# Branch b's projection as a seven-product Strassen multiplication

## The chip, the cores and the metric

The kernel runs on one core of one Trainium2 chip. The metric is the device time of one execution in microseconds (us), the median of several runs. The engines are named as in the profile: PE is the matrix engine (TensorE), PEld its weight load, DVE the vector engine, ACT the scalar engine, POOL the GpSimd engine, SP the engine whose queue issues most loads.

## The reference

One layer of a token mixer with a channel mixer, on 512 latent tokens of width 1024, with 256 context tokens that only feed the starting states of a gated linear attention. Cut to what matters here:

```python
u, vs, q, r, ga, gb, k, v, lr = _split(h @ w_in, IN_SPLITS)
a = _spatial_gating(gelu(u), gelu(vs), sgu_ln_g, sgu_ln_b, sgu_w, sgu_b)
o, s_f, s_b = _gla_bidir(...)                                   # 512 x 1024, 4 heads
o = o * rsqrt(mean(o * o) + EPS)                                # per head
o = o.reshape(...) * gla_norm_g                                 # one gain per column
ob = o * silu(r)
merged = sigmoid(ga) * (a @ w_br_a) + sigmoid(gb) * (ob @ w_br_b)
x = x + g1x * (merged @ w_o)
hx2 = _modulate(_rms_norm(x, norm2_g), sh2x, sc2x)              # h * (1 + scale) + shift
x = x + g2x * _conv_ffn(hx2, ...)
```

`sh2x`, `sc2x`, `g1x` and `g2x` are columns of `silu(c) @ w_ada + b_ada`, called modulations. Everything is in 32-bit floats.

## The kernel before, in words

**Precision.** Each operand of a large product is split into a high part (rounded by ACT, as `wh`, `ah`, `mh`) and a remainder (by DVE, as `wl`, `al`, `ml`), and each product is three matmuls: high by high, high by remainder, remainder by high. A weight tile is 128 x 1024: two row blocks of 512 columns, or eight row blocks of 128.

**Stages.** After the attention, the kernel runs one large product after another on PE: `u`, then `vs` (the shift branch of the spatial gating), gate a (`ga`), branch a's projection (`w_br_a`), gate b (`gb`), gate r (`r`), branch b's projection (`w_br_b`), the output product (`w_o`), then the channel mixer. Within each, tokens come in four tiles of 128 and columns in two halves `hf` of 512.

**Two ways to multiply 512 x 1024 by 1024 x 1024.** `wide_tm` is the plain way: for one column half, all four token tiles, then token tile by token tile for the other half (`wide_step`, L462). `strassen` (L517) splits tokens, inner dimension and columns in halves and makes seven products of quarters in the order a11, s3, s2, a12, s1, a22, s4, where s1 to s4 are sums of quarters of the left operand. Each of the seven takes two weight tiles, for two token tiles each; after each weight tile it calls `step()`, so steps 1 to 14 stand for the 14 weight tiles. `done(hf, t, source, sign)` is called for each finished output tile: (0, 0) and (0, 1) after a12, (1, 2) and (1, 3) after s1, (0, 2) and (0, 3) after a22, (1, 0) and (1, 1) after s4. With `low_first`, a12 comes after a22. In this kernel `vs`, `ga`, `gb`, `r` and `w_o` are Strassen products and `w_br_b` is a plain one.

**Weights.** `specs` is the list of weight tiles in the order of use, `loads` their DMAs; `weights(lead, ahead)` hands out the next tile, splits up to `lead` tiles further and issues loads up to `ahead` tiles further. `w_cols` is a plain tile; with `scaled` it is multiplied by the norm's gain `gng` while it is split (L201 on ACT, L202 on DVE). `w_strassen` makes the 14 tiles of a Strassen product, whose weight quarters also have to be added: `tt` holds b22 + b12, summed by an accumulating DMA from POOL (L230); t2 adds b11 to it (L274, L276 on DVE), and t4 adds b21 by a second accumulating DMA. There are five buffers each for raw weights, `wh` and `wl`.

**Around branch b.** `r_done` makes `ob` as `silu(r)` times the normalized attention output `os_` and puts a `turn` on a list `todo`: four transposes on PE (L1456), a copy on ACT and a remainder on DVE (L431, L432). `br_b_done` multiplies a finished tile by gate b, adds branch a (L1563, L1564) and puts an `mg_turn` on the list: four transposes (L1535), then the quarter sums s1 to s4 of the merged operand that `w_o`'s Strassen product needs, each split. `do()` takes turns from the list at chosen steps.

**Modulations.** `ada2` makes a modulation vector: 256 KB tiles of `w_ada` are multiplied by a column of `c` and added up on DVE (L1318), 16 such steps for each of scale, shift and the two gates; then PE sums over the partitions (L1337 for columns). It is a generator; `sc_tick` runs one piece of the second modulation's scale at a chosen step. Eight of its 16 sums run in `vs`, and the other eight and the column sums in branch b.

Pools: `heap` has 44 tiles of 128 x 512, `late` 27, PSUM two pools (`mm`, `gl`) of four banks. Instructions are put in order on each engine by a scheduler at compile time that follows the order of the program unless an operand isn't ready in its own plan of the times.

Of the kernel before, what the change touches and what calls it, by code (L numbers as in the profile page):

```python
# [8 lines left out]
F32 = mybir.dt.float32  # L9
# [7 lines left out]
P = 128  # L17
# [16 lines left out]
def backbone_kernel(  # L34
# [19 lines left out]
    def nm(s):  # L54
        cnt[0] += 1
        return f"{s}_{cnt[0]}"
# [10 lines left out]
    def mm():  # L67
        return pm.tile([P, 512], F32, tag="mm", name=nm("mm"))
# [110 lines left out]
            V.tensor_tensor(hl[1].tiles[i], part, hl[0].tiles[i].bitcast(F32), op=ALU.subtract)  # L179
        return hl  # L180

    def w_cols(w, c0, n=P, k0=0, kn=KT, scaled=False, ahead=False):
        ap = w[k0 * P:(k0 + kn) * P, c0:c0 + n].rearrange("(k p) c -> p k c", p=P)
        held = []

        def load():
            held.append(raw_tile(kn, n))
            dma(held[0], ap)
            last_load["cols"] = traced()[-1].name

        def split():
            if ahead:
                return split_heap(held.pop())
            if not scaled:
                return split_new(held.pop(), kn, n)
            raw = held.pop()
            wh = wp.tile([P, kn, n], F32R, tag="wh", name=nm("wh"))
            wl = wp.tile([P, kn, n], F32R, tag="wl", name=nm("wl"))
            for kk in range(kn):
                g_ = gng[:, k0 + kk:k0 + kk + 1]  # L200
                A.mul(wh[:, kk, :], raw[:, kk, :], g_)  # L201
                V.scalar_tensor_tensor(wl[:, kk, :], raw[:, kk, :], g_, wh[:, kk, :].bitcast(F32), op0=ALU.mult,  # L202
                                       op1=ALU.subtract)
            return wh, wl

        loads.append((len(specs), load))
        specs.append(split)

    def w_wide(w, scaled=False):
        for hf in range(2):  # L210
            for k in range(KT // 2):
                w_cols(w, hf * 512, 512, 2 * k, 2, scaled)

    def w_strassen(w, c0, add_b12=False, low_first=False, pool=heap):

# [23 lines left out]
        def load_t(j):  # L239
            def load():  # L240
                tt[j] = [pool([P, 512], s="tt") for _ in range(2)]
                start = len(traced())
                for kk in range(2):
                    dma(tt[j][kk], blk(1, 1, j)[kk * P:(kk + 1) * P, :])
                if low_first:
                    behind(start, last_load["cols"])
                add_rows(j, 0, 1)
            return load

# [75 lines left out]
            w_cols(w_br_a[0], hf * 512, 512, 2 * k, 2)  # L325
    w_strassen(wi, O_GB)
    w_strassen(wi, O_R)
    w_wide(w_br_b[0], scaled=True)
    w_strassen(w_o[0], 0, True, True, late)
    for f in range(FT):  # L330
        w_cols(ffn_w_up[0], f * P)
# [126 lines left out]
    def wide_step(ps, w, acts, t, k):  # L458
        wh, wl = w
        ah, al = acts(k, t)  # L460
        for i, (a, b) in enumerate(((ah, wh), (ah, wl), (al, wh))):
            T.matmul(ps, a, b[:, k % 2, :], start=(k == 0 and i == 0), stop=(k == KT - 1 and i == 2))  # L462

    def of_cols(acts):
        return lambda k, t: [z[:, t * P:(t + 1) * P] for z in acts[k]]

    def of_blocks(acts):
        return lambda k, t: [z[:, (k % 4) * P:(k % 4 + 1) * P] for z in acts[t, k // 4]]

    def wide_half(hf, pss, acts, done, step, lead=4, ahead=AHEAD):  # L470
        for k2 in range(KT // 2):
            w = weights(1, ahead)
            for kk in range(2):
                for t in range(4):
                    wide_step(pss[t], w, acts, t, 2 * k2 + kk)
                step()
            if k2:
                stream_split(pos[2] + min(k2 + 1, lead))
        for t in range(4):
            done(hf, t, pss[t])  # L480

    def wide_tm(acts, done, step, order=(0, 1, 2, 3)):

        wide_half(0, [mm() for _ in range(4)], acts, done, step)
        ws = [weights() for _ in range(KT // 2)]
        for t in order:
            ps = (mm if t != order[0] else gl)()
            for k in range(KT):
                wide_step(ps, ws[k // 2], acts, t, k)
            done(1, t, ps)  # L490
            step()
            step()

    def wide_all(acts, done, step):

# [804 lines left out]
    bc_g = {}  # L1300
    cols = {}

    ada_bank = [gl]

    def ada2(kinds):
        cs0 = {"g1": 2048, "sh": 3072, "sc": 4096, "g2": 5120}
# [108 lines left out]
    def ga_step():  # L1415
        slots[0] += 1
        n = slots[0] - 6
        if -3 <= n <= 0:
            vs_norm(n + 3)
        if 0 <= n < KT:  # L1420
            sgu_part(n)
        if n >= KT:
            a_split()
# [20 lines left out]
    wide_all(lambda k, t: [z[:, t * P:(t + 1) * P] for z in a_act[k]], br_a_done, br_a_step)  # L1444
    a_act.clear()
    ug.clear()
    ada_bank[0] = mm

    todo = []

    def turn(src, dst, key, bank, lo_pool=heap):

        def go():
            ps = bank()
            for kk in range(4):
                T.transpose(ps[:, kk * P:(kk + 1) * P], src[:, kk * P:(kk + 1) * P], ident)  # L1456
            dst[key] = split_act(ps, s="tr", eng=A.copy, lo_pool=lo_pool)
        return go

    def do(n=1):  # L1460
        for _ in range(n):
# [29 lines left out]
    for i in [i for i in traced()[start:] if i.engine == V.engine][:12]:  # L1491
        tc.add_manual_dep(i, low_banks[-1], mybir.DependencyInfo(
            mybir.DependencyClass.NoSync, mybir.DependencyReason.DATA), reason="low_banks")
    ada_bank[0] = gl

    ob = {}

    def r_done(hf, t, src, sign):
        sr = heap([P, 512], s="sr")
        A.activation(sr, src, AF.Silu, scale=sign)  # L1500
        V.tensor_tensor(sr, os_[t][hf], sr, op=ALU.mult)
        todo.append(turn(sr, ob, (t, hf), mm if hf == 0 and t < 2 or hf and t > 1 else gl))

    count = [0]

    def r_step():
        count[0] += 1
        if count[0] > 10:
            do()

    strassen(of_sums, r_done, r_step)
    hx.clear()
    sums.clear()
    do(len(todo) - 2)

    mg, mf = {}, {}

    def mg_turn(t, hf):

        s_, u, f_ = gb[t][hf], t % 2, lambda z: z.bitcast(F32)  # L1520

        def split(name, src, scale=1.0):
            hi, lo = heap([P, 512], F32R, s="mh"), heap([P, 512], F32R, s="ml")
            if scale == 1.0:
                A.copy(hi, src)
                V.tensor_tensor(lo, src, f_(hi), op=ALU.subtract)
            else:
                A.mul(hi, src, scale)
                V.scalar_tensor_tensor(lo, src, scale, f_(hi), op0=ALU.mult, op1=ALU.subtract)
            mg[name, u] = hi, lo  # L1530

        def go():
            ps = gl()
            for kk in range(4):
                T.matmul(ps[:, kk * P:(kk + 1) * P], s_[:, kk * P:(kk + 1) * P], ident, is_transpose=True,  # L1535
                         start=kk == 0, stop=kk == 3, skip_group_check=True)
            if t > 1 and hf == 0:
                mf["a21", u] = heap([P, 512], s="mf")
                A.copy(mf["a21", u], ps)
            elif hf == 0:  # L1540
                mf["a11", u] = heap([P, 512], s="mf")
                A.copy(mf["a11", u], ps)
                split("a11", ps)
                d = heap([P, 512], s="ms")
                V.tensor_tensor(d, ps, mf["a21", u], op=ALU.subtract)
                split("s3", d)
            elif t > 1:
                split("a22", ps)
                d, q = mf.pop(("a21", u)), mf["a11", u]
                V.tensor_tensor(d, ps, d, op=ALU.subtract)  # L1550
                V.tensor_tensor(q, q, d, op=ALU.add)
                split("s2", q, -1.0)
                split("s1", d)
            else:
                split("a12", ps)
                q = mf.pop(("a11", u))
                V.tensor_tensor(q, q, ps, op=ALU.subtract)
                split("s4", q)
        return go

    def br_b_done(hf, t, ps):
        s_ = gb[t][hf]
        V.tensor_tensor(s_, ps, s_, op=ALU.mult)  # L1563
        V.tensor_tensor(s_, s_, br[t][hf], op=ALU.add)  # L1564
        if hf:
            todo.append(mg_turn(t, hf))
        elif t > 1:
            todo.extend([mg_turn(t, 0), mg_turn(t - 2, 0)])

    count[0] = 0  # L1570

    def br_b_step():
        count[0] += 1
        if count[0] > 1:
            do()
        if 8 < count[0] < 12:
            stream_split(pos[2] + count[0] - 7)
        if count[0] < 5:
            for _ in range(2):
                sc_tick()  # L1580
        if count[0] == 7:
            for _ in range(3):
                sc_tick()

    wide_tm(of_blocks(ob), br_b_done, br_b_step, (2, 0, 3, 1))
    drain()
    am2 = const([P, 8], "am2")
    V.tensor_scalar(am2, cols["sc"], 1.0, None, op0=ALU.add)
    V.tensor_tensor(am2, am2, n2g, op=ALU.mult)
# [104 lines left out]
    def wo_step():  # L1694
        count[0] += 1
        if count[0] == 1:
            x1_load()
            table_for(AF.Sqrt)
        if count[0] == 14:
            low_later.append(later)  # L1700
            stream_split(pos[2] + 4)
            low_later.clear()
        do()

    strassen(lambda name, k, t: [z[:, k * P:(k + 1) * P] for z in mg[name, t]], wo_done, wo_step, True)


    gact, s12, s4 = [], [], []
# [373 lines left out]
```

## Time and profile before

| | |
|---|---|
| median of 3 runs | 908.41 us (907.97 to 908.92) |
| profiled execution, its own time | 908.53 us |
| its span, first to last instruction | 906.8 us |
| mean granted clock | 0.997 |
| PE busy | 892.1 us, 98% |
| DVE busy | 755.7 us, 83% |
| ACT busy | 477.4 us, 53% |
| POOL busy | 80.9 us, 9% |
| HBM read | 135.52 MB |

The span is the profiled execution from its first instruction to its last; the execution's own time is some 1.7 us longer. Stages by the start of their PE work: `vs` 249.6, gate a 290.0, branch a 335.3, gate b 378.8, gate r 419.8, branch b 460.6, `w_o` 510.5. In the rows of the profile, `out<-in` names the tile written and those read, `x12` is a count, and a bracket after a row is the idle time ahead of it and what ended it.

### The profile page before, as it was taken

The numbers are of one execution on the slowest core, as the hardware profiler recorded it, in microseconds if no ns is written. First come the engines' busy times: TensorE is split into PE (matmuls) and PEld (weight loads), VectorE is DVE, ScalarE is ACT, GpSimd is POOL, SyncE is SP. The second block draws the span as 40 slices with busy tenths as digits, with TensorE's granted clock in tenths as the row PEclk, the third lists the DMA queues.
The fourth block names the chain that finished last, engine by engine and source line by source line (L and its number), as shares of the span: only waits on it lengthen the run. The fifth ranks groups of instructions, "written<-read, shape, count | busy, mean of one in ns | idle before, by whom it ended". The sixth has DMA issues, their size and how long they took to land.

```text
span 906.8 us, 12638 instructions
## 1 busy us (share of the span) xinstructions
PE 892.1 (98%) x4527; PEld 745.7 (82%) x4527; DVE 755.7 (83%) x1312; ACT 477.4 (53%) x846; POOL 80.9 (9%) x114
## 2 busy tenths in 40 slices
PE   6999999999999999999999999999999999999996
PEld 5778888888888888888888889888888888888885
DVE  5668777899999778796686986899999888999796
ACT  5146454767465742475652568533333343466574
POOL 3000000001121010021020100000000000123003
PEclk9999999999999999999999999999999999999998
DMA  9961401026875668699576633263444333399522
GB/s 270 330 177 30 118 22 48 25 70 191 198 202 159 162 190 295 200 263 254 167 210 186 148 90 112 71 198 116 136 132 128 105 93 116 96 236 252 141 76 93
DMA packets 127068, 138.44 MB, mean 153 GB/s; under 512 B 7402, under 2 KB 82486, under 8 KB 127006
## 3 DMA queue, kind: packets, MB, share of 16 engines
q1 hardware_dynamic: 115197, 118.38, 41.3%
q0 software_dynamic: 10368, 18.57, 12.3%
q8 instruction: 35, 0.57, 0.3%
q10 hardware_dynamic: 1440, 0.69, 0.3%
q14 instruction: 28, 0.22, 0.1%
HBM read 135.52 MB, written 2.10 MB: 152 GB/s over the span
## 4 chain that ended last, share of the span: by engine, by line
PE 96%; DVE 2%; ACT 1%; DMA 0%; issue 0%; ACTq 0%; DVEq 0%
PE mm L439 29%; PE gl L517 12%; PE mm L462 9%; PE mm L517 9%; PE gl L1857 7%; PE mm L1857 5%; PE gl L439 4%; PE gl L462 3%; PE mm L454 3%; PE mm L762 3%; PE gl L982 2%; PE gl L762 1%; PE mm L1152 1%; PE mm L1091 1%; PE gl L685 1%; PE gl L1018 1%
## 5 line engine op out<-in xcount | busy, mean ns | idle before, releaser
L164 ACT CAST wh<-raw 128x1024 fp32r<-128x1024 f32 x107 | 111.8, 1051 | 105.2 <-PE mm L439 65.9
L165 DVE TENSOR_TENSOR wl<-raw,wh 128x1024 fp32r<-128x1024 f32 x107 | 130.0, 1219 | 21.1 <-ACT wh L164 19.3
L1740 DVE SCALAR_TENSOR_TENSOR cacc<-ca,ccol,cacc 128x441 f32<-128x441 f32 (+2 forms) x176 | 120.9, 693 | 6.1 <-ACT cacc L1728 2.8
L439 PE MATMUL mm<-h2h,wh 128*128 128x512 f32 x320 | 124.6, 389 | 0.0
L439 PE MATMUL mm<-h2h,wl 128*128 128x512 f32 x320 | 124.6, 389 | 0.0
L439 PE MATMUL mm<-h2l,wh 128*128 128x512 f32 x320 | 124.6, 389 | 0.0
L439 PEld LDWEIGHTS mm<-h2l,wh 128*128 128x128 f32 x320 | 60.1, 188 | 12.5
L439 PEld LDWEIGHTS mm<-h2h,wh 128*128 128x128 f32 x320 | 60.1, 188 | 12.4
L439 PEld LDWEIGHTS mm<-h2h,wl 128*128 128x128 f32 x320 | 60.1, 188 | 12.4
L1318 DVE SCALAR_TENSOR_TENSOR acc<-wa,c_col,acc 128x512 f32<-128x512 f32 x64 | 46.0, 747 | 4.6 <-DMA wa<-in_w_ada_dram 4.0
L1743 ACT ACTIVATE cacc<-cacc 128x512 f32<-128x512 f32 x22 | 13.9, 633 | 58.7 <-DVE cacc L1740 58.6
L230 POOL DMA_DIRECT2D tt<-in_w_in_dram x32 | 27.9, 998 | 174.5 <-DMA tt<-in_w_in_dram 57.5
L264 DVE TENSOR_TENSOR wl<-tt,wh 128x512 fp32r<-128x512 f32 x56 | 36.4, 683 | 7.6 <-ACT wh L263 7.6
L263 ACT CAST wh<-tt 128x512 fp32r<-128x512 f32 x56 | 32.6, 620 | 18.2 <-DVE tt L276 3.9
L517 PE MATMUL mm<-wh,hxh 128*128 128x512 f32 x96 | 38.0, 395 | 0.0
L517 PE MATMUL mm<-wh,hxl 128*128 128x512 f32 x96 | 37.4, 390 | 0.0
L517 PE MATMUL mm<-wl,hxh 128*128 128x512 f32 x96 | 37.4, 389 | 0.0
L1779 POOL DMA_DIRECT2D b<-in_ffn_w_down_dram x11 | 9.5, 888 | 283.4 <-DMA b<-in_ffn_w_down_dram 256.8
L1799 ACT CAST wh<-raw 128x1024 fp32r<-128x1024 f32 x22 | 23.1, 1053 | 15.9 <-PE mm L1857 4.7
L1800 DVE TENSOR_TENSOR wl<-raw,wh 128x1024 fp32r<-128x1024 f32 x22 | 26.8, 1218 | 4.5 <-ACT wh L1799 4.4
L517 PE MATMUL gl<-wh,xh 128*128 128x512 f32 x64 | 25.5, 399 | 0.0
L517 PE MATMUL gl<-wh,xl 128*128 128x512 f32 x64 | 24.9, 390 | 0.0
(552 smaller groups left out, 2398.0 us busy)
## 6 DMA issues: line engine op xcount, KB each, us to landing
raw<-in_w_in_dram SPq DMA_DIRECT2D x54, 512.0 KB
wa<-in_w_ada_dram SPq DMA_DIRECT2D x96, 256.0 KB
raw<-in_ffn_w_up_dram SPq DMA_DIRECT2D x44, 512.0 KB
raw<-in_ffn_w_down_dram SPq DMA_DIRECT2D x22, 512.0 KB
tt<-in_w_in_dram POOLq DMA_DIRECT2D x32, 256.0 KB, 6.8
tt<-in_w_in_dram SPq DMA_DIRECT2D x16, 256.0 KB
raw<-in_w_br_a_dram SPq DMA_DIRECT2D x8, 512.0 KB
raw<-in_w_br_b_dram SPq DMA_DIRECT2D x8, 512.0 KB
```

The lines of the kernel that those rows point to most:

```text
L164: A.copy(wh, raw)
L165: low = lambda: V.tensor_tensor(wl, raw, wh.bitcast(F32), op=ALU.subtract)
L230: G.dma_start(tt[j][kk], blk(kh, nh, j)[kk * P:(kk + 1) * P, :], accum_op=ALU.add)
L263: A.copy(wh[:, kk, :], tt[j][kk])
L264: V.tensor_tensor(wl[:, kk, :], tt[j][kk], wh[:, kk, :].bitcast(F32), op=ALU.subtract)
L439: T.matmul(ps, a[:, k, :], b[:, c0:c0 + n], start=(k == 0 and i == 0), stop=(k == KT - 1 and i == 2))
L462: T.matmul(ps, a, b[:, k % 2, :], start=(k == 0 and i == 0), stop=(k == KT - 1 and i == 2))
L517: T.matmul(ps[t], a, b[:, kk, :], start=(first and i == 0), stop=(j == 1 and kk == 1 and i == 2), skip_group_check=again)
L762: T.matmul(fps[i], a, b, start=(k == 0 and z == 0), stop=(k == KT - 1 and z == 2))
L1318: V.scalar_tensor_tensor(a_, w_, c_col[:, k:k + 1], a_, op0=ALU.mult, op1=ALU.add)
L1740: V.scalar_tensor_tensor(o, a_[:, r0 + dy:r1 + dy, c0 + dx:c1 + dx], wcol(tap), o, op0=ALU.mult, op1=ALU.add)
L1857: T.matmul(ps, a[:, t * P:(t + 1) * P], w[b][:, j, c0:c0 + n], start=(first and i == 0), stop=(last and i == 2), skip_group_check=again)
```

## The change

`w_br_b` becomes a Strassen product. Its weights are no longer scaled by the norm's gain: the gain is put on the turned operand, where its columns lie on the partitions. One new function, `sums_turn`, takes the place of `turn` and `mg_turn`: it transposes one quarter (a11, a22, a21 or a12, for token tile u), with the gain if one is given, and makes the splits of the quarters and sums s1 to s4 as soon as their parts are there. Both branch b and `w_o` take their operands from it. Turns run at steps 10 to 14 (a11, a11, a22, a22, both a21) of gate r and of branch b, and at step 5 (both a12) of the product that follows. The scale's remaining eight sums and its column sums move to steps 1, 2, 4, 5 and 6 of gate a. The later loads of `w_o`'s `tt` are put behind the last quarter of `w_br_b`.

```diff
-    w_wide(w_br_b[0], scaled=True)
+    w_strassen(w_br_b[0], 0)
...
     def ga_step():
         slots[0] += 1
         n = slots[0] - 6
+        for _ in range({1: 3, 2: 3, 4: 2, 5: 1, 6: 1}.get(slots[0], 0)):
+            sc_tick()
...
+    def sums_turn(dst, name, u, src, scale=None):
...
+        def split(n_, raw, c=1.0):
+            hi, lo = heap([P, 512], F32R, s="mh"), heap([P, 512], F32R, s="ml")
+            if c == 1.0:
+                A.copy(hi, raw)
+                V.tensor_tensor(lo, raw, f_(hi), op=ALU.subtract)
+            else:
+                A.mul(hi, raw, c)
+                V.scalar_tensor_tensor(lo, raw, c, f_(hi), op0=ALU.mult, op1=ALU.subtract)
+            dst[n_, u] = hi, lo
 
         def go():
-            ps = bank()
+            ps = mm()
             for kk in range(4):
                 T.transpose(ps[:, kk * P:(kk + 1) * P], src[:, kk * P:(kk + 1) * P], ident)
-            dst[key] = split_act(ps, s="tr", eng=A.copy, lo_pool=lo_pool)
+            raw = ps
+            if scale is not None or name in ("a11", "a22"):
+                raw = heap([P, 512], s="mf")
+                if scale is None:
+                    A.copy(raw, ps)
+                else:
+                    for kk in range(4):
+                        A.mul(raw[:, kk * P:(kk + 1) * P], ps[:, kk * P:(kk + 1) * P], scale[:, kk:kk + 1])
+            if name in ("a11", "a22"):
+                dst["raw", name, u] = raw
+                split(name, raw)
+            elif name == "a21":
+                q, d = kept("a11"), kept("a22")
+                s3 = heap([P, 512], s="ms")
+                V.tensor_tensor(s3, q, raw, op=ALU.subtract)
+                split("s3", s3)
+                V.tensor_tensor(d, d, raw, op=ALU.subtract)
+                V.tensor_tensor(q, q, d, op=ALU.add)
+                split("s2", q, -1.0)
+                split("s1", d)
+                dst["raw", "q", u] = q
+            else:
+                split("a12", raw)
+                q = kept("q")
+                V.tensor_tensor(q, q, raw, op=ALU.subtract)
+                split("s4", q)
         return go
...
-        V.tensor_tensor(sr, os_[t][hf], sr, op=ALU.mult)
-        todo.append(turn(sr, ob, (t, hf), mm if hf == 0 and t < 2 or hf and t > 1 else gl))
+        V.tensor_tensor(os_[t][hf], os_[t][hf], sr, op=ALU.mult)
+        todo.append(sums_turn(ob, *turn_names(hf, t), os_[t][hf], gng[:, 4 * hf:4 * hf + 4]))
...
+    turns = {10: 1, 11: 1, 12: 1, 13: 1, 14: 2}
...
-    def br_b_done(hf, t, ps):
+    def br_b_done(hf, t, src, sign):
         s_ = gb[t][hf]
-        V.tensor_tensor(s_, ps, s_, op=ALU.mult)
-        V.tensor_tensor(s_, s_, br[t][hf], op=ALU.add)
...
+        V.tensor_tensor(s_, src, s_, op=ALU.mult)
+        if sign > 0:
+            V.tensor_tensor(s_, br[t][hf], s_, op=ALU.add)
+        else:
+            V.tensor_tensor(s_, br[t][hf], s_, op=ALU.subtract)
+        todo.append(sums_turn(mg, *turn_names(hf, t), s_))
...
+    late_turns = {5: 2}
...
-        if count[0] < 5:
-            for _ in range(2):
-                sc_tick()
-        if count[0] == 7:
-            for _ in range(3):
-                sc_tick()
...
-    wide_tm(of_blocks(ob), br_b_done, br_b_step, (2, 0, 3, 1))
+    strassen(of_turned(ob), br_b_done, br_b_step)
```

More of the change, by code (lines that the diff above doesn't have):

```diff
@@ L180, in split_heap, with w_cols @@
         return hl
-    def w_cols(w, c0, n=P, k0=0, kn=KT, scaled=False, ahead=False):
+    def w_cols(w, c0, n=P, k0=0, kn=KT, ahead=False):
         ap = w[k0 * P:(k0 + kn) * P, c0:c0 + n].rearrange("(k p) c -> p k c", p=P)
@@ L193, in split @@
                 return split_heap(held.pop())
[L194 to L204, printed above, removed]
+            return split_new(held.pop(), kn, n)
         loads.append((len(specs), load))
         specs.append(split)
[L209 to L212, printed above, removed]
     def w_strassen(w, c0, add_b12=False, low_first=False, pool=heap):
@@ L245, in load @@
                 if low_first:
-                    behind(start, last_load["cols"])
+                    behind(start, last_load["b22"])
                 add_rows(j, 0, 1)
@@ L462, in wide_step @@
             T.matmul(ps, a, b[:, k % 2, :], start=(k == 0 and i == 0), stop=(k == KT - 1 and i == 2))
[L464 to L492, printed above, removed]
     def wide_all(acts, done, step):
@@ L1301, in backbone_kernel @@
     cols = {}
-    ada_bank = [gl]
+    ada_bank = [mm]
     def ada2(kinds):
@@ L1446, in backbone_kernel, with turn_names @@
     ug.clear()
-    ada_bank[0] = mm
     todo = []
-    def turn(src, dst, key, bank, lo_pool=heap):
+    ob, mg = {}, {}
+    def sums_turn(dst, name, u, src, scale=None):
+        f_ = lambda z: z.bitcast(F32)
+        kept = lambda n_: dst.pop(("raw", n_, u))
+        def split(n_, raw, c=1.0):
[7 more added lines that the diff above has]
+            dst[n_, u] = hi, lo
         def go():
-            ps = bank()
+            ps = mm()
             for kk in range(4):
                 T.transpose(ps[:, kk * P:(kk + 1) * P], src[:, kk * P:(kk + 1) * P], ident)
-            dst[key] = split_act(ps, s="tr", eng=A.copy, lo_pool=lo_pool)
-        return go
+            raw = ps
[24 more added lines that the diff above has]
+                split("s4", q)
+        return go
+    def turn_names(hf, t):
+        return (("a11", "a21"), ("a12", "a22"))[hf][t // 2], t % 2
     def do(n=1):
@@ L1493, in backbone_kernel @@
             mybir.DependencyClass.NoSync, mybir.DependencyReason.DATA), reason="low_banks")
-    ada_bank[0] = gl
-    ob = {}
     def r_done(hf, t, src, sign):
@@ L1500, in r_done @@
         A.activation(sr, src, AF.Silu, scale=sign)
-        V.tensor_tensor(sr, os_[t][hf], sr, op=ALU.mult)
-        todo.append(turn(sr, ob, (t, hf), mm if hf == 0 and t < 2 or hf and t > 1 else gl))
+        V.tensor_tensor(os_[t][hf], os_[t][hf], sr, op=ALU.mult)
+        todo.append(sums_turn(ob, *turn_names(hf, t), os_[t][hf], gng[:, 4 * hf:4 * hf + 4]))
     count = [0]
+    turns = {10: 1, 11: 1, 12: 1, 13: 1, 14: 2}
     def r_step():
         count[0] += 1
-        if count[0] > 10:
-            do()
+        do(turns.get(count[0], 0))
     strassen(of_sums, r_done, r_step)
@@ L1513, in backbone_kernel @@
     sums.clear()
[L1514 to L1559, printed above, removed]
@@ L1561, in br_b_done @@
-    def br_b_done(hf, t, ps):
-        s_ = gb[t][hf]
-        V.tensor_tensor(s_, ps, s_, op=ALU.mult)
-        V.tensor_tensor(s_, s_, br[t][hf], op=ALU.add)
[L1565 to L1568, printed above, removed]
+    def br_b_done(hf, t, src, sign):
+        s_ = gb[t][hf]
+        V.tensor_tensor(s_, src, s_, op=ALU.mult)
[4 more added lines that the diff above has]
+        todo.append(sums_turn(mg, *turn_names(hf, t), s_))
@@ L1570, in backbone_kernel @@
     count[0] = 0
+    late_turns = {5: 2}
     def br_b_step():
         count[0] += 1
[L1574 to L1577, printed above, removed]
-        if count[0] < 5:
-            for _ in range(2):
-                sc_tick()
-        if count[0] == 7:
-            for _ in range(3):
-                sc_tick()
-    wide_tm(of_blocks(ob), br_b_done, br_b_step, (2, 0, 3, 1))
-    drain()
+        do((turns if count[0] > 9 else late_turns).get(count[0], 0))
@@ L1587, in backbone_kernel @@
+    of_turned = lambda dst: lambda name, k, t: [z[:, k * P:(k + 1) * P] for z in dst[name, t]]
+    strassen(of_turned(ob), br_b_done, br_b_step)
+    ob.clear()
+    ada_bank[0] = gl
     am2 = const([P, 8], "am2")
@@ L1702, in wo_step @@
             low_later.clear()
-        do()
-    strassen(lambda name, k, t: [z[:, k * P:(k + 1) * P] for z in mg[name, t]], wo_done, wo_step, True)
+        do(late_turns.get(count[0], 0))
+    strassen(of_turned(mg), wo_done, wo_step, True)
     gact, s12, s4 = [], [], []
```

## The prediction

> **What bounds the kernel now.** I read the page's busy shares and its chain first, then the chain of branch b's stretch in order of time, then that stretch by windows.
>
> ```profile
> span 906.8 us, 12638 instructions
> PE 892.1 (98%) x4527; PEld 745.7 (82%) x4527; DVE 755.7 (83%) x1312; ACT 477.4 (53%) x846; POOL 80.9 (9%) x114
> PE 96%; DVE 2%; ACT 1%; DMA 0%; issue 0%; ACTq 0%; DVEq 0%
> ```
>
> PE is the bound: 98% busy, 96% of the chain. Only fewer PE instructions, or PE waits, can move the end. The chain from gate r to the output product w_o (start, length, what):
>
> ```profile
> 419.78 10.88 PE mm L517 x48
> 459.75 0.87 PE gl L1456 x8
> 460.62 2.06 PE mm L462 x9
> 462.68 0.04 issue
> 470.12 10.93 PE mm L462 x48
> 481.05 1.68 PE gl L1337 x16
> 491.07 0.87 PE gl L1535 x8
> 510.10 0.44 PE gl L1535 x4
> 510.54 3.68 PE mm L517 x16
> 528.09 10.90 PE gl L517 x48
> ```
>
> L517 is a Strassen product, L462 branch b's plain one, L1456 and L1535 the two kinds of turn, L1337 the scale's column sums. All of it is PE; the one wait is 0.04 us. 48 products last 10.88 us in Strassen form and 10.93 in plain form: 0.2267 us each. By windows (the stages shift norm vs, gate a, r, branch b, w_o; columns: length, PE, weight loads, DVE, ACT, POOL, granted clock, DMA share, GB/s), and last the densest DVE stretch of b and w_o:
>
> ```profile
> 249.62:289.98 40.36, 40.36 (x176) 32.60 (x175) 39.43 (x66) 23.59 (x37) 6.93 (x8) 1.00 0.69 189
> 289.98:335.32 45.34, 45.34 (x234) 38.71 (x233) 38.97 (x59) 31.15 (x45) 5.61 (x9) 1.00 0.57 164
> 419.78:460.62 40.84, 40.84 (x194) 33.99 (x193) 27.01 (x37) 26.83 (x42) 3.49 (x4) 1.00 0.67 189
> 460.62:510.54 49.92, 49.88 (x246) 41.42 (x245) 39.86 (x66) 20.65 (x37) 8.34 (x9) 1.00 0.66 168
> 510.54:549.20 38.66, 38.66 (x174) 31.89 (x174) 32.66 (x50) 25.48 (x42) 2.04 (x4) 1.00 0.47 132
> 491.83:524.49 32.66, 32.66 (x158) 27.18 (x157) 29.95 (x46) 19.59 (x34) 4.49 (x6) 1.00 0.47 114
> ```
>
> See two things: the clock is 1.00 throughout, and DVE is second everywhere. In vs it is 97.7% busy (39.43 of 40.36) and PE still waits for nothing; in b and w_o its densest stretch reaches 29.95/32.66 = 92%.
>
> **The change part by part.** Prices of single instructions (mean ns after the comma):
>
> ```profile
> L165 DVE TENSOR_TENSOR wl<-raw,wh 128x1024 fp32r<-128x1024 f32 x107 | 130.0, 1219 | 21.1 <-ACT wh L164 19.3 <-PE gl L1007 1.4
> L264 DVE TENSOR_TENSOR wl<-tt,wh 128x512 fp32r<-128x512 f32 x56 | 36.4, 683 | 7.6 <-ACT wh L263 7.6
> L202 DVE SCALAR_TENSOR_TENSOR wl<-raw,vec_b,wh 128x512 fp32r<-128x512 f32 x16 | 11.8, 747 | 6.4 <-ACT wh L201 6.4
> L1318 DVE SCALAR_TENSOR_TENSOR acc<-wa,c_col,acc 128x512 f32<-128x512 f32 x64 | 46.0, 747 | 4.6 <-DMA wa<-in_w_ada_dram 4.0 <-DVE acc L1318 0.2
> L201 ACT ACTIVATE wh<-raw,vec_b 128x512 fp32r<-128x512 f32 x16 | 11.4, 722 | 13.9 <-PE mm L462 8.6 <-issue 2.8 <-PE gl L517 1.7
> L1481 ACT ACTIVATE os<-o,var 128x256 f32<-128x256 f32 x16 | 7.3, 502 | 9.6 <-DVE acc L1318 9.6
> L431 ACT CAST trh<-mm 128x512 fp32r<-128x512 f32 x4 | 2.3, 567 | 0.0
> ```
>
> *1. The product.* Plain: 8 row blocks x 4 token tiles x 2 halves x 3 = 192 matmuls. Strassen: 7 products x 4 row blocks x 2 token tiles x 3 = 168. So 24 x 0.2267 = **-5.44 us**. In sentences the sum does not use: the Trainium skill (TensorE: Matmul & The Clock Gate, "Back-to-back issue gap") gives about 131 ns for a sustained 512-column matmul behind its weight load; by that the saving would be only about 3.1 us, an estimate from that page. The trace disagrees (48 in 10.88 us), so I keep 227 ns.
>
> *2. Turns and column sums.* Eight turns of branch b's operand and eight of the merged one stand before and after, four transposes each: 0.44 us for x4, 0.87 for x8, in either form. The column sums (1.68 us) move from b to gate a, where PE is as full. Both 0.
>
> *3. Scale sums in gate a.* Eight multiply-adds (L1318), two column copies, 16 column matmuls and eight 256 KB loads move there, on SP's queue ahead of later weights. Back to back a multiply-add takes about 0.67 us, 5.4 in all: DVE goes from 38.97 of 45.34 to 44.7 of 47.0, 95%, under the 97.7% that vs bears without a PE wait. The loads add 2 MB to a stage at 164 GB/s; vs took the same eight at 189. What waits anew is PE: the column matmuls stand at steps 5 and 6 right behind the last sums, with the gate's products queued behind them. Bounds 0 (the lead of the weights covers it) to 1 us; I take 0, being nearest to vs.
>
> *4. Weights of b.* Out: 16 scaled casts on ACT (L201) and 16 scaled remainders on DVE (L202). In: 14 weight tiles, four row sums on POOL's accumulating queue and four more later, 7 MB instead of 4. A direct precedent is the passage from gate b to r, the same weight scheme:
>
> ```profile
> 409.34 1.23 DVE L274 TENSOR_TENSOR raw<-raw,raw 128x1024 f32<-128x1024 f32 x1 [0.92 <-DMA raw<-in_w_in_dram]
> 417.80 1.29 DVE L264 TENSOR_TENSOR wl<-tt,wh 128x512 fp32r<-128x512 f32 x2 [0.74 <-ACT wh L263]
> 419.01 1.29 DVE L276 TENSOR_TENSOR tt<-tt,raw 128x512 f32<-128x512 f32 x2
> 423.24 1.29 DVE L264 TENSOR_TENSOR wl<-tt,wh 128x512 fp32r<-128x512 f32 x2 [0.98 <-ACT wh L263]
> tt<-in_w_in_dram POOLq DMA_DIRECT2D x32, 256.0 KB, 6.8
> SPq L224 <- DVE tt L276: 29.8, 4, 17.7
> ```
>
> r begins at 419.78, and by then the weight sums of its third product are made (409, 419) and their last remainder is done at 424.5; it is needed at 433. An accumulating load lands 6.8 us after issue and is asked for six weights (16 us) ahead. So DMA and POOL: 0, bounded above by one late load, 4.5 us.
>
> *5. The turn of the third quarter (a21), r's end.* PE makes two turns (0.87), then the first product (24 x 0.2267 = 5.44), then needs s3 of token tile 0 at +6.3 and of tile 1 at +7.7. The norm's scale costs four 128x128 multiplies on ACT: 256 columns cost 502, 512 cost 722, so 128 about 390, some 0.30 back to back, 1.3 us a turn. ACT: silu 0.5, four multiplies to 1.8, four to 3.1, casts of 0.57; DVE 0.6 apiece: both s3 are whole at about +5.4. If instead the queues run tile 0's three splits before tile 1's multiplies, tile 1 comes at +9.4 (remainder due +8.1): 1.3 us. I take 0, the merged operand's turns having left no wait at 510-528.
>
> *6. The last quarter (a12), step 5 of branch b.* Between its transposes and its use lie one step (2.72) plus the second turn (0.44): 3.16 us for tile 0, 4.5 for tile 1. ACT needs 0.5 + 1.3 + 0.57 = 2.4, then again 1.9: 4.3, plus up to 1.05 if a weight cast stands between. Bounds 0 to 1.0: I take **+0.5**.
>
> *7. DVE from r's last product to w_o's step 5.* PE: 0.87 + 38.1 + six turns at 0.44 = 41.6, then five steps and the turns before: 14.5; 56.1 us. DVE in that time, operations of 512 columns: gate r's last 2, a21 12, a12 6, t4 4, t2's remainders 4, Strassen adds 4, merge 16, the merged operand's a11, a22 4 and a21 12, w_o's first weights 8 and t2 8: 80. At 0.605 (two take 1.29) 48.4, and six of 1024 at 1.14, 6.8: 55.2. Four remainders (s1, a22) are due later: 52.8, or 94%. At vs's 97.7% that fits; at 92% it ends at 57.4, 1.3 late. I take **+0.8**. If t2's sums were not made early in r: 55.2 + 4 x 0.605 + 2 x 1.14 = 59.9, at 92% 65.1: 9.0 late. So 0 to 9.0. w_o's tail has 6 us of DVE to spare (32.66 of 38.66) for the seven operations that arrive later.
>
> **Sum:** -5.44 + 0.5 + 0.8 = -4.1. The profiled execution took 908.53 (906.8 and 1.7 outside the span), 0.12 over the median of 908.41: the forecast is **904.3**.
>
> **The rivals.** *A, everything is covered:* 908.41 - 5.44 = 903.0. For it: no PE wait anywhere from gate b to w_o now, and vs at 97.7%. Against: steps 6 and 7 each lack about 1 us at their upper ends.
>
> *B, the turns run in tile order:* 1.3 at r's end, the same at w_o's start, 1.0 at step 6: -5.44 + 3.6, 906.6. For it: ACT has eight multiplies more at r's end than today. Against: early work fills gaps, as at 419.01.
>
> *C, slower: DVE falls behind in branch b.* One mechanism: t2's sums are not made in r but inside b, so the s2 and a12 operands of w_o come late at step 5. Full price -5.44 + 9.0: 912.0. It decides when DVE is more than 7.2 us late there; from 3.6 it eats the gain. For it: the ledger's 94 to 107%. Against: r leaves DVE 27.01 of 40.84, and the precedent made the sums early. A PE gap would also cost clock by the Trainium skill (same page, "The HAM clock gate"): about 3.4 us of idling halves it, by estimate up to 1.7 us more; no run here shows such a gap, and the rows read 1.00.
>
> *D, branch b's weights come late:* raw buffers are freed by DVE, and SP's queue stands behind them (29.8 us in four waits). One late load: 904.3 + 4.5 = 908.8, same or just slower. Against: those waits cost PE nothing today.
>
> **How the numbers follow.** Forecast 0.40, A 0.23, B 0.13, C 0.14, D 0.10. 0.2% (1.8 us, 906.6 and 910.2) is about what a measurement of this kernel tells from no change. Faster: 0.40 + 0.23 + most of B, 0.11 = 0.74. Same: 0.02 of B, 0.06 of C where it stops short, 0.05 of D: 0.13. Slower: 0.08 + 0.05 = 0.13. The range goes from A less 0.2 to just short of D, 902.8 to 908.4, leaving out C and most of D; the likeliest case alone is 903.6 to 905.4.
>
> **What would show it.** L462 in branch b gone, 168 matmuls of L517 in its place in about 41 us with turns. The chain between r and w_o all PE but for under 2 us, lying at the seventh weight of branch b (ACT, a12) and in w_o's second or third product (DVE). Gate a longer by 1.7 us of column sums with no PE wait; DVE near 95% in gate a, branch b and w_o's first half. Wrong if PE waits over 3.6 us for DVE in w_o (C), if a wait on a weight tile whose releaser is a DMA shows (D), or if w_o's tail ends late because DVE is.

## The result and the profile after

The changed kernel takes 914.43 us (median), the kernel before 908.66 us on the same chip: 1.0064 of it, 95% interval 1.0052 to 1.0076, so 5.8 us slower (4.7 to 6.9 by that interval). The PE work shrank as forecast, and PE stood still for longer than it saved. The page of the changed kernel, its first lines and its chain:

```profile
span 912.1 us, 12690 instructions
PE 890.6 (98%) x4503; PEld 740.1 (81%) x4503; DVE 775.4 (85%) x1340; ACT 496.7 (54%) x894; POOL 88.1 (10%) x122
PE 43%; DVE 3%; ACT 2%; DMA 1%; issue 0%; DVEq 0%; ACTq 0%
```

4527 PE instructions became 4503: the 24 matmuls are gone. But the chain, 96% PE before, now leaves PE. Followed back from the end, it stays with PE as far as w_o; from there back it alternates between PE and long DVE stretches, and it begins at a load issued at 459 us. Two pieces of it in order of time (start, length, what), branch b's start and w_o's. Line numbers are those of each kernel's own file. In this one L472 is a matmul of a Strassen product and L1425 a turn's transposes; L1415, L1416, L1418 and L1419 split a quarter or a sum of the operand; L1440, L1442 and L1443 make s3, s1 and s2; L248, L249 and L261 are the cast, the remainder and t2's sum of a weight tile `tt`; L490 is the copy of a PSUM bank behind the product s2.

```profile
459.19 7.47 DMA tt<-in_w_br_b_dram
466.65 0.02 issue
466.68 1.14 ACT wh L248 x2
467.82 0.53 ACT mh L1415
468.35 0.02 issue
468.37 0.69 DVE ml L1416
...
512.28 0.60 DVE ms L1440
512.87 0.60 DVE mf L1442
513.47 0.60 DVE tt L261
514.08 0.60 DVE ml L1416
...
518.29 0.61 DVE ms L1440
518.90 0.02 issue
518.92 0.63 ACT mh L1415
```

Branch b starts at 464.4, and a row sum of its weights (`tt`) lands only at 466.7. In w_o, s3 of token tile 0 (`ms` L1440) is made at 512.3 and that of tile 1 at 518.3, with the rest of tile 0's turn and four operations on weights (`tt`, `wl`) in between. The stages by windows (vs, gate a with its sums, r, branch b, w_o; columns as in the prediction):

```profile
250.31:290.51 40.20, 40.20 (x176) 32.42 (x174) 39.18 (x65) 23.51 (x37) 6.93 (x8) 1.00 0.76 209
290.51:339.11 48.60, 47.38 (x250) 40.39 (x248) 44.44 (x71) 31.15 (x45) 5.27 (x8) 1.00 0.62 179
423.57:464.41 40.84, 40.84 (x194) 33.76 (x192) 27.25 (x35) 28.39 (x52) 7.01 (x8) 1.00 0.67 167
464.41:509.34 44.93, 42.98 (x204) 34.51 (x202) 43.45 (x67) 33.34 (x65) 9.33 (x10) 1.00 0.85 222
509.34:553.40 44.06, 41.38 (x180) 31.85 (x177) 41.88 (x66) 30.72 (x51) 4.46 (x6) 1.00 0.60 149
```

The stages meet at the first instruction of the next stage's product here; w_o ends at the first transposes of the second norm (553.40; 549.04 before). Against the kernel before:

| stage | before | after | difference | what it is |
|---|---|---|---|---|
| gate a | 45.33 | 48.60 | +3.3 | 1.7 column sums moved in, 1.4 a wait, the rest gaps beside them |
| gate b, gate r | 81.7 | 81.8 | 0 | |
| branch b | 49.91 | 44.93 | -5.0 | 5.4 fewer matmuls, 1.7 column sums out, 0.4 a turn out; 2.6 lost in waits |
| w_o | 38.75 | 44.06 | +5.3 | 0.4 a turn in; 4.9 in waits and in products out of order |
| norm and first channel-mixer products | 26.69 | 27.83 | +1.1 | a wait of 0.8 for DVE, with its gap 1.0 |

The differences add up to 4.8 us. The profiled executions differ by 5.3 (913.82 against 908.53); `vs` begins 0.7 us later in the changed one (250.31 against 249.62), behind work that the change does not touch.

What PE waited for between 285 and 560 us, the four largest of seven rows (in total, times, longest), and the largest of the waits for the copy L490:

```profile
PE mm L472 <- ACT mh L1415: 2.1, 2, 1.2
PE gl L472 <- ACT gl L490: 1.4, 2, 1.0
PE mm L1292 <- ACT vr L1344: 1.2, 1, 1.2
PE gl L1571 <- DVE yt L1587: 0.8, 1, 0.8
531.71 0.50 PE L472 MATMUL gl<-wh,mh 128*128 128x512 f32 x1 [1.03 <-ACT gl L490]
```

ACT is named in three, but read the rows of ACT and DVE too. At the longer of the two waits for `mh` (1.2 us, w_o) ACT had itself been idle until DVE gave it s3 at 518.9; at the other (1.0 us, branch b) DVE gave the sum at 474.5 and ACT first cast a weight tile, until 475.4. In gate a the row names `vr`, whereas the last scale sum of the first column half, the first of the pair below, ended on DVE at about 305.4, just before PE went on at 305.49. Ahead of it DVE had stood idle for 1.26 us, because the load for the sixth sum was late:

```profile
300.57 0.75 DVE L1273 SCALAR_TENSOR_TENSOR acc<-wa,c_col,acc 128x512 f32<-128x512 f32 x1 [1.26 <-DMA wa<-in_w_ada_dram]
304.65 1.40 DVE L1273 SCALAR_TENSOR_TENSOR acc<-wa,c_col,acc 128x512 f32<-128x512 f32 x2
```

### The profile page after: what moved, and what is told of

It is laid out like the page before. It is cut to its first block, busy times and chain, and to the rows that moved or that the text cites. A ratio compares the mean times of both kernels' runs of the same rounds, so it can differ in the third digit from the quotient of the medians.

```text
span 912.1 us, 12690 instructions
## 1 busy us (share of the span) xinstructions
PE 890.6 (98%) x4503; PEld 740.1 (81%) x4503; DVE 775.4 (85%) x1340; ACT 496.7 (54%) x894; POOL 88.1 (10%) x122
## 5 line engine op out<-in xcount | busy, mean ns | idle before, releaser
L164 ACT CAST wh<-raw 128x1024 fp32r<-128x1024 f32 x115 | 120.1, 1051 | 110.9 <-PE mm L424 62.4
L165 DVE TENSOR_TENSOR wl<-raw,wh 128x1024 fp32r<-128x1024 f32 x115 | 139.4, 1218 | 20.9 <-ACT wh L164 20.5
L248 ACT CAST wh<-tt 128x512 fp32r<-128x512 f32 x68 | 39.9, 621 | 20.2 <-PE mm L472 8.5
L249 DVE TENSOR_TENSOR wl<-tt,wh 128x512 fp32r<-128x512 f32 x68 | 44.5, 681 | 5.6 <-ACT wh L248 5.5
L472 PE MATMUL mm<-wh,hxh 128*128 128x512 f32 x96 | 37.9, 395 | 0.0
L472 PE MATMUL mm<-wh,hxl 128*128 128x512 f32 x96 | 37.4, 389 | 0.0
L472 PE MATMUL mm<-wl,hxh 128*128 128x512 f32 x96 | 37.4, 389 | 0.0
L1741 ACT CAST wh<-raw 128x1024 fp32r<-128x1024 f32 x22 | 23.0, 1052 | 14.9 <-PE mm L1799 4.4
L1742 DVE TENSOR_TENSOR wl<-raw,wh 128x1024 fp32r<-128x1024 f32 x22 | 26.8, 1219 | 4.5 <-ACT wh L1741 4.4
L472 PE MATMUL gl<-wh,mh 128*128 128x512 f32 x64 | 25.9, 405 | 1.9 <-ACT gl L490 1.4
L472 PE MATMUL gl<-wh,xh 128*128 128x512 f32 x64 | 25.6, 400 | 0.0
```

What stands on the lines that cost most here:

```text
L164: A.copy(wh, raw)
L165: low = lambda: V.tensor_tensor(wl, raw, wh.bitcast(F32), op=ALU.subtract)
L248: A.copy(wh[:, kk, :], tt[j][kk])
L249: V.tensor_tensor(wl[:, kk, :], tt[j][kk], wh[:, kk, :].bitcast(F32), op=ALU.subtract)
L472: T.matmul(ps[t], a, b[:, kk, :], start=(first and i == 0), stop=(j == 1 and kk == 1 and i == 2), skip_group_check=again)
L1742: V.tensor_tensor(wl, raw, wh.bitcast(F32), op=ALU.subtract)
```

## The experiments

Four kernels ran beside the kernel before on one chip, then four more, then four; each ratio is against the kernel before of its own group, and kernel 1 is the kernel of experiment 1, and so on. Three questions were put: did branch b's weight sums come late (theory T), has DVE simply too much work there (W), or is ACT with its 32 new multiplies the cause (A)? Later also: does the order inside the turns cost (O)?

**1. Branch b's `tt` in the other pool.**

```diff
-    w_strassen(w_br_b[0], 0)
+    w_strassen(w_br_b[0], 0, pool=late)
```

> Changes against the changed kernel: branch b's tt tiles come from the pool late (27 tiles) instead of heap (44). Theory T (late sums): tt found no free tile in heap until the shift of gate r freed some, so its load left at 451 us, its last row sum landed at 466.7 and t2's four sums on DVE fell into branch b (465 to 476) instead of gate r. Then the load goes out ahead of 445, the sums are made in gate r, DVE has 2.4 to 4.8 us less to do in branch b, and of the 8.4 us of PE waits in branch b and w_o 3 to 5 go: 909.5 to 911.5. Theory W (too much DVE work in all, whenever the weights come): the sums move, but the rest still fills DVE; under 1.5 us come back: 913 to 914.5. Theory A (ACT's multiplies): no change, 914.

Measured 911.09 against 909.03: 1.0026 (1.0015 to 1.0036). From 1.0064, some 3.4 us came back, in theory T's range. The loads of `tt` (SP's queue) and their sums (POOL's queue), first in the changed kernel and then in this one:

```profile
451.01 1.88 SPq L229 DMA_DIRECT2D tt<-in_w_br_b_dram  x4
457.23 3.52 POOL L215 DMA_DIRECT2D tt<-in_w_br_b_dram  x4 [27.30 <-PE gl L472]
```

```profile
409.71 2.69 SPq L229 DMA_DIRECT2D tt<-in_w_br_b_dram  x4
420.45 1.84 POOL L215 DMA_DIRECT2D tt<-in_w_br_b_dram  x2 [8.95 <-DVE tt L261]
422.53 1.75 POOL L215 DMA_DIRECT2D tt<-in_w_br_b_dram  x2 [0.25 <-DMA tt<-in_w_br_b_dram]
```

In the changed kernel `tt` stood on SP's queue behind five raw tiles of the same product. With another pool and nothing else changed the load goes 41 us earlier, so what it lacked was a free tile of `heap`. Two of t2's four sums now run before branch b starts, the other two still inside it. Branch b falls from 44.93 to 42.61 us, so the profile gives the late load 2.3 us. The rest of the 3.4 stands in stages ahead of the loads that this edit moves: `vs` begins 0.6 us earlier, and the wait for the column sums in gate a was 0.6 us in this execution, not 1.2. w_o does not move (44.05): its 4.9 us have another cause.

**2. Without the gain on the turned operand.** The norm's gain is left out, so its result is another one.

```diff
-        todo.append(sums_turn(ob, *turn_names(hf, t), os_[t][hf], gng[:, 4 * hf:4 * hf + 4]))
+        todo.append(sums_turn(ob, *turn_names(hf, t), os_[t][hf]))
```

> Changes against the changed kernel: the norm's gain is left out on the turned operand of branch b, so the 32 multiplies of 128 x 128 on ACT go (a11 and a22 are one copy each, a21 and a12 are read from PSUM): some 6.8 us less ACT work, DVE's operations the same in number. Theory A (ACT is late at the turns): most of the waits whose releaser is ACT go, 3 to 5 us back: 909.5 to 911.5. Theories T and W (DVE is late, ACT stands behind it): at most 1.5 us, 913 to 914.5.

1.0077 (1.0062 to 1.0092): no better than with the multiplies. Theory A falls: with 32 multiplies fewer on ACT the two waits for `mh` were 3.5 us instead of 2.1, and w_o stayed at 43.7 us. The edit also lets DVE read two of the quarters from PSUM, and behind the longer wait, 2.6 us, the granted clock fell to half for some 3.4 us, so its time is not the price of the multiplies alone.

**3. The scale sums alone.** The kernel before, with the sums of branch b moved to gate a, their PSUM pool set as in the changed kernel, and nothing else.

```diff
...
+        for _ in range({1: 3, 2: 3, 4: 2, 5: 1, 6: 1}.get(slots[0], 0)):
+            sc_tick()
...
-        if count[0] < 5:
-            for _ in range(2):
-                sc_tick()
-        if count[0] == 7:
-            for _ in range(3):
-                sc_tick()
```

> The kernel before with one part of the change alone: the remaining eight scale sums and the column sums moved from branch b to gate a. PE work is the same in all. If the wait of 1.4 us for the column sums at step 5 of gate a belongs to this part alone, gate a gets 3.3 us longer (1.7 of column sums, 1.6 of waits), branch b 1.7 shorter, and the time is 1.4 to 1.8 us over before: 910.0 to 910.6. If that wait came from the changed kernel's other parts: 908.5, within 0.5.

1.0018 (1.0007 to 1.0029), 1.6 us over before. Its only PE wait in the stretch is the first row here; the second is the window behind it (columns as before, the granted clock third from the end):

```profile
PE mm L1337 <- ACT vr L1389: 1.2, 1, 1.2
306.00:310.00 4.00, 4.00 (x15) 3.22 (x13) 2.48 (x4) 0.81 (x2) 0.00 (x0) 0.57 0.85 271
```

So this part costs its wait by itself, with branch b's product still the plain one. In this profiled execution it cost more: soon after the wait the clock fell to half for some 3.4 us, a matmul of 512 columns took 0.43 us instead of 0.23, and gate a lost 1.4 us to that besides the 1.4 of the wait and its gap.

**4. The merge's additions on POOL.**

```diff
-            V.tensor_tensor(s_, br[t][hf], s_, op=ALU.add)
+            G.tensor_tensor(s_, br[t][hf], s_, op=ALU.add)
...
-            V.tensor_tensor(s_, br[t][hf], s_, op=ALU.subtract)
+            G.tensor_tensor(s_, br[t][hf], s_, op=ALU.subtract)
```

> Changes against the changed kernel: branch b's eight merges with branch a (add or subtract, 128 x 512) go from DVE to POOL, which takes about 1.3 us for such an operation (DVE 0.68). DVE loses 4.8 us of work between the a12 product of branch b and the start of w_o. Theory W (DVE work in all): w_o's waits shrink by 3 to 5 us, branch b's stay: 909.5 to 911.5. Theory T: the arrears are made before step 5 of branch b; 1 to 3 us come back in w_o: 911.5 to 913.5. Theory A: no change, 914; slower if POOL's longer latency lies ahead of the turns.

1.0087 (1.0070 to 1.0104): worse. Here two of them took 3.0 to 3.4 us, not 2.6, and a turn now waited for POOL (1.6 us). It says nothing on W; experiment 9 shows why.

**5. s3 of both tiles first.** On kernel 1; the same operations in another order.

```diff
...
                 split("s3", s3)
-                V.tensor_tensor(d, d, raw, op=ALU.subtract)
-                V.tensor_tensor(q, q, d, op=ALU.add)
-                split("s2", q, -1.0)
-                split("s1", d)
+                rests.append((split, q, d, raw))
                 dst["raw", "q", u] = q
+                if u:
+                    for sp, q, d, raw in rests:
+                        V.tensor_tensor(d, d, raw, op=ALU.subtract)
+                        V.tensor_tensor(q, q, d, op=ALU.add)
+                        sp("s2", q, -1.0)
+                    for sp, q, d, raw in rests:
+                        sp("s1", d)
+                    rests.clear()
```

> Changes against the kernel with branch b's tt tiles in late (2 us over before, 908.6 us of span): in the turns of the third quarter, both token tiles' s3 are made first, then both s2, then both s1; the same operations in another order. Theory O (order: w_o waits for s3 of tile 1, which stands behind s2 and s1 of tile 0): the 1.3 us wait at the second product of w_o goes, and the products that were pulled ahead of it stand in order again; w_o gets 2 to 4 us shorter, the time 1 to 2 us under before. Theory W (DVE has too much work up to step 5 of w_o in any order): the wait moves to s2 or the adds; w_o at most 1 us shorter, 1 to 2 us over before.

909.65 against 908.94: 1.0005 (0.9996 to 1.0014), level with before and some 2 us under kernel 1. The wait for s3 of tile 1 is gone, but in the profile w_o is only 0.4 us shorter (43.66), branch b 0.5. What PE waits for now in w_o is the next thing on DVE, and behind that wait the clock again fell to half:

```profile
PE gl L472 <- DVE wl L249: 1.0, 1, 1.0
517.00:521.00 4.00, 4.00 (x11) 3.14 (x12) 3.92 (x7) 2.73 (x4) 1.74 (x2) 0.57 0.84 189
```

The slow clock stretched w_o's products by some 1.6 us; without it w_o would be about 2 us shorter, by estimate, which is what the medians say and the low end of theory O. What is left in w_o, the wait for `wl`, is W's.

**6. b12 + b11 by an accumulating load.** On kernel 1.

```diff
-    w_strassen(w_br_b[0], 0, pool=late)
+    w_strassen(w_br_b[0], 0, True, pool=late)
```

> Changes against the kernel with branch b's tt tiles in late: the sum b12 + b11 of branch b's weights is made by an accumulating load on POOL's queue, and two DVE operations of 128 x 1024 (1.14 us each) go. Theory W: 2.3 us less DVE work in the filled stretch give 1.5 to 2.5 us back, within 0.5 us of before. Theory O: both operations lie in gate r, where DVE is not full, and nothing comes back: 1.5 to 2.5 us over before. If the added load lands late (6 to 7 us after issue), 1 us worse.

1.0025 (1.0016 to 1.0034), against kernel 1's 1.0026: nothing. These two operations lay in gate r, where DVE has time.

**7. The column sums two steps later.** On kernel 1.

```diff
-        for _ in range({1: 3, 2: 3, 4: 2, 5: 1, 6: 1}.get(slots[0], 0)):
+        for _ in range({1: 3, 2: 3, 4: 2, 7: 1, 8: 1}.get(slots[0], 0)):
```

> Changes against the kernel with branch b's tt tiles in late: the scale's two column sums stand at steps 7 and 8 of gate a instead of 5 and 6. If PE's wait there (0.8 to 1.4 us) is for the last multiply-adds alone, 5.4 us of additional time lets them finish: the wait goes and the time falls by 0.8 to 1.4 us, to 0.5 to 1.5 us over before. If DVE is too full in gate a as a whole, the wait moves to the spatial gating's tiles, and the time stays at 2 us over.

1.0023 (1.0013 to 1.0033). The wait did not go, it moved to the spatial gating's tiles, which DVE must empty before PE can write them:

```profile
PE mm L1352 <- DVE ug L1357: 1.6, 1, 1.6
```

**8. The three together** (5, 6 and 7 on kernel 1).

> The three changes together on the kernel with branch b's tt tiles in late. Theory O and the column sums: 3 to 5 us less than that kernel, 1 to 3 us under before (0.1 to 0.3%). Theory W: 3 to 4 us less, from the weight sum rather than the order. If neither holds: within 1 us of before or over it.

909.18 against 908.94: 1.0002 (0.9993 to 1.0010). Level with before; of the 1 to 3 us under it, none. Branch b is now 42.34 us with no wait, against 42.4 by the table; w_o is still 43.08.

**9. Two merges on POOL, far from their use.** On kernel 8.

```diff
         if sign > 0:
             V.tensor_tensor(s_, br[t][hf], s_, op=ALU.add)
+        elif t < 2:
+            G.tensor_tensor(s_, br[t][hf], s_, op=ALU.subtract)
```

> On the kernel with the three changes together (level with before): the last two subtractions of branch b's merge, whose turns come only at step 5 of w_o, go from DVE to POOL. They stand right ahead of s3 on DVE, where PE waits. Theory W (from branch b's start to w_o's step 5 DVE is busy 95% and sets the pace): 1.2 us less DVE work there, 0.8 to 1.5 us back, 0.1% under before. If POOL's queue, which also issues accumulating loads that wait, holds them up: PE waits at step 5 of w_o, 1 us or more worse.

1.0007 (0.9998 to 1.0016): nothing back. Their results are needed some 15 us later, and nobody waits for them. But look at DVE while POOL runs (505.99 to 509.34):

```profile
505.99 3.35 POOL L1522 TENSOR_TENSOR sgb<-br,sgb 128x512 f32<-128x512 f32 x2 [4.71 <-DVE sgb L1518]
507.17 1.01 DVE L1418 TENSOR_TENSOR ml<-mf,mh 128x512 fp32r<-128x512 f32 x1
508.11 2.38 DVE L239 TENSOR_TENSOR ph<-tt,ph 128x512 fp32r<-128x512 f32 x2
```

The remainder takes 1.01 us instead of 0.68 and the pair 2.38 instead of 1.29: DVE lost 1.4 us beside POOL, as much as the two operations it was spared. Kernel 12 shows the same two lengths.

**10. The merge without branch a.** On kernel 8; branch a's contribution is left out, so the result is another one.

```diff
-        if sign > 0:
-            V.tensor_tensor(s_, br[t][hf], s_, op=ALU.add)
-        else:
-            V.tensor_tensor(s_, br[t][hf], s_, op=ALU.subtract)
```

> On the kernel with the three changes together: branch a's contribution is left out of the merge, so eight DVE operations (4.8 us) between branch b's a12 product and w_o's start go, and nothing takes their place. Theory W: w_o's waits, some 4 us, shrink by 3 to 4, and the stretch from branch b to w_o's end falls to within 1.5 us of its PE work; 3 to 4 us under before (0.3 to 0.45%). If w_o's waits come from something else (weights, PSUM banks, the scheduler's order): under 1 us, level with before.

0.9990 (0.9981 to 0.9999), about 1.1 us under kernel 8, though the two intervals overlap. In the profile w_o falls from 43.08 to 41.18 us, and the wait for `wl` L249 (1.2 there) is gone; half of what W foretold. Two waits stay as they were, the copy behind s2, and the norm's bank just after w_o:

```profile
PE gl L472 <- ACT gl L490: 1.0, 1, 1.0
PE gl L1574 <- DVE yt L1590: 0.8, 1, 0.8
```

**11. The scale sums in gate r.** On kernel 8, out of gate a and into steps 1 to 4, 8 and 9 of gate r.

```diff
-        for _ in range({1: 3, 2: 3, 4: 2, 7: 1, 8: 1}.get(slots[0], 0)):
-            sc_tick()
...
+        for _ in range({1: 2, 2: 2, 3: 2, 4: 2, 8: 1, 9: 1}.get(count[0], 0)):
+            sc_tick()
         do(turns.get(count[0], 0))
```

> On the kernel with the three changes together: the scale's eight sums and two column sums stand at steps 1 to 4, 8 and 9 of gate r, where DVE is busy 27 of 41 us, instead of in gate a. If gate a's wait is DVE's load there, it goes, with none in gate r: 1.0 to 1.5 us back, 0.1% under before. If gate r then makes fewer of branch b's weight sums early, branch b loses what gate a gains: level with before.

908.49 against 908.81: 0.9994 (0.9985 to 1.0003). Gate a is back at the time of the kernel before, gate r takes 1.9 us more, 1.7 of them the column sums, and branch b stays as in kernel 8; the 0.7 us between the medians lie within the noise (gate a, r, branch b, w_o):

```profile
289.94:335.27 45.33, 45.33 (x233) 38.70 (x232) 39.45 (x60) 31.20 (x45) 4.85 (x7) 1.00 0.57 163
419.74:462.43 42.69, 42.69 (x210) 35.63 (x208) 33.13 (x50) 29.98 (x56) 9.36 (x10) 1.00 0.83 205
462.43:504.71 42.28, 42.28 (x204) 34.30 (x202) 40.85 (x63) 31.85 (x62) 9.35 (x10) 1.00 0.92 238
504.71:547.80 43.09, 40.43 (x180) 32.18 (x179) 41.73 (x66) 30.72 (x51) 4.48 (x6) 1.00 0.57 144
```

**12. Both.** Kernels 9 and 11 together.

> Both: the scale's sums in gate r and the last two merges on POOL. If both hold, 2 to 3 us under before (0.2 to 0.3%): the version that would beat both kernels. If one fails, 1 us under; if both, level or slower.

908.76 against 908.81: 0.9995 (0.9986 to 1.0004), no better than 11 alone. The best of all, kernel 11, is some 6 us under the changed kernel, and against the kernel before its interval holds 1: no version here is shown to beat that.

## Why the prediction was wrong

The sign was wrong. What came is rival C's mechanism, given 0.14: t2's sums are not made in gate r but inside branch b, and DVE falls behind. Three smaller losses stand beside it. By steps:

*1, the product.* Right. 24 matmuls are gone, and without waits branch b takes 42.3 us (kernel 11), as 49.91 less 5.4, 1.7 and 0.4 gives 42.4. The 5.4 us are 24 matmuls at 0.227 us each. The 131 ns that the Trainium skill gives (TensorE: Matmul & The Clock Gate, "Back-to-back issue gap") did not show.

*2, turns and column sums.* Right: nothing but their moving.

*3, scale sums in gate a.* Put at 0 with an upper bound of 1 us; gate a lost 1.6 us beyond the column sums, 1.4 of them one wait and its gap. DVE's work came out as forecast, 44.44 us busy for 44.7. What the step left out is when the loads arrive: the stage's rate was counted, not the place of these loads on SP's queue, where they stood behind a weight load that waited 8.2 us for DVE. DVE then idled for the sixth sum's load, and the more it idled the longer PE waited for the column sums: 0.72 and 0.46 us in kernel 5, 0.96 and 0.61 in kernel 1, 1.26 and 1.22 in the changed kernel, 1.59 and 1.34 in kernel 6. With the column sums two steps later (experiment 7) DVE idled 1.54 us there and PE waited 1.55 a little further on; in gate r (kernel 11) both are gone. That the load is the cause is read from these rows; no run changed the load alone.

*4, weights of b.* Here the forecast failed first. The precedent, gate b to gate r, was the same scheme of weights but not the same moment of the pool: in that passage `tt` was loaded 20 us ahead of its stage, in this one 13, for want of a free tile in `heap`. I counted loads, bytes and queues and no tiles. Taken at 0 with one late load, 4.5 us, as the bound; the profile of experiment 1 gives 2.3 us.

*5, the turn at r's end and at w_o's start.* The order feared in rival B was there, tile 0 whole before tile 1, and cost most at w_o's start. B's 3.6 us were too many: the order is worth some 2 us (experiment 5).

*6, the last quarter.* 0.5 taken; one wait of 0.4 stood there in the changed kernel, named for the copy behind s2 and not for a12's cast, and none at all in kernel 8. Right in size.

*7, DVE's ledger.* This is the term that was most mis-sized: +0.8 taken, 5.6 us measured. It took from step 4 that t2's sums would be made in gate r. The stretch is the one from r's last transposes to those of a12 in w_o; here it is in the changed kernel, in kernels 1, 8 and 10:

```profile
463.62:527.68 64.06, 60.78 (x276) 47.44 (x275) 61.06 (x95) 44.59 (x84) 11.94 (x13) 1.00 0.76 192
462.45:524.22 61.77, 60.36 (x277) 47.45 (x275) 59.36 (x92) 43.44 (x82) 11.96 (x13) 1.00 0.76 194
462.37:522.79 60.42, 58.96 (x275) 47.34 (x274) 58.58 (x91) 43.51 (x81) 11.96 (x13) 1.00 0.77 195
463.36:521.82 58.46, 58.44 (x276) 47.44 (x275) 54.04 (x83) 43.66 (x81) 11.96 (x13) 1.00 0.79 201
```

Kernel 10 waits for nothing here and takes 58.46 us, not the 56.1 of the sum: the transposes stood behind 67 of w_o's matmuls, where the sum had 60. Against that the changed kernel is 5.6 us late, kernel 1 with the earlier load 3.3, and kernel 8 with the new order and the weight sum by load 2.0; the last 2.0 go with the merge's eight additions. So the 5.6 are DVE's work and its place, part by part. Its unit price was right and its count was not: the changed kernel ran 95 operations here, 88 of 512 columns and 7 of 1024, against 80 and 6. The nine more are t2's four sums, three weight remainders, a turn's remainder and one wide remainder; 8 x 0.605 + 1.14 = 6.0, the difference of 61.06 and 55.2. DVE reached 95%. C's bound was 9.0 us late.

So the sum is, in its own terms: -5.4 + 5.6 in that stretch + 1.6 in gate a + 1.9 in w_o behind the stretch + 1.1 after w_o, the 4.8 us of the stages. The last two were in no term. The 1.9 in w_o are a wait of 0.3 for a weight's cast and the 1.0 for the copy behind s2, with their gaps. As for the loss after w_o, the list of DVE's work ended at step 5, and "6 us to spare in w_o's tail" was read from a w_o whose start had not been filled. At its end two weight remainders (2.35 us) stand ahead of the gate's multiply that frees the norm's bank:

```profile
552.22 2.35 DVE L165 TENSOR_TENSOR wl<-raw,wh 128x1024 fp32r<-128x1024 f32 x2
554.49 1.28 DVE L1587 TENSOR_TENSOR yt<-gl,g 128x512 f32<-128x512 f32 x2
```

The price that rival C put on a PE gap, half the clock, was not paid in the changed kernel's profiled execution: its windows above read 1.00. It was paid in five of the twelve experiments' profiled executions (2, 3, 4, 5 and 9), each time for some 3.4 us and 1.4 to 1.6 us of matmul time, near the 1.7 of the estimate. The idling was much shorter than the 3.4 us that the Trainium skill's rule (TensorE: Matmul & The Clock Gate, "The HAM clock gate") names: one wait of 1.2 us in experiment 3, one of 1.3 in experiment 9. Waits as long in the changed kernel (1.2) and in kernel 7 (1.6) left the clock at 1.00, so what decides is open.

What stays open: w_o is 4.3 us longer than before even in kernel 11 (43.09). 0.4 of that is a turn, and experiment 10 shows 1.9 to be DVE's work. The remaining 2 us, the waits for a weight's cast and for the copy behind s2, outlived it. Why ACT's copy comes late there, weight casts being queued ahead of it, was argued from the order of the rows and not tried.

## What to carry to other kernels

When a product is replaced by a cleverer one with fewer matmuls, write the ledger of the engine that makes its operands, and give each cheap item its place: "made ahead, as in the stage before" holds only if a free tile, a free queue and time stand there at that moment. Count the tiles of the pool at the passage, not only the bytes and the operations. The busy share alone does not decide: DVE at 97.7% left no wait in `vs`, at 92% none in kernel 10's stretch, and at 95 to 97% it cost 2.0 to 5.6 us in the others. What decides is whether each result is there when the first engine reaches it. A saving on the first engine comes back only as far as the second has been relieved or put in the right order.

## What the runs showed of the hardware

POOL's 128x512 additions are no free help for DVE. Two of them took 3.35 us on POOL, and DVE's operations meanwhile stretched from 0.68 to 1.01 us and from 1.29 to 2.38 us, so that sparing DVE two operations (1.2 us) saved no time. Not every operation stretched: one that reads PSUM, at 506.56 in the same execution, took 0.69 us beside POOL.

A wait of PE as short as 1.2 us can be followed by some 3.4 us at half the granted clock, as in experiment 3, and an equal wait can be followed by none, as in the changed kernel. One profiled execution can so hide a gain that the medians show, as in experiment 5.

And a wait's named releaser need not be the cause: PE waited "for ACT" in gate a and at the turns, but taking 32 multiplies off ACT gave nothing back (1.0077), while order and earlier sums on DVE did.
